# How the low part of 84 weight slabs is formed: a subtraction on GpSimd, or a transfer that adds onto the negated rounded weight

## The chip, the cores and the metric

The kernel runs on one core of a Trainium2 chip. The metric is the device time of one execution, in microseconds (us); the kernel before takes 781.51 us, the median of three runs. The engines are named as in the profile: PE (TensorE, matrix products; PEld is its weight load), DVE (VectorE), ACT (ScalarE), POOL (GpSimd) and SP (SyncE, which issues the loads and stores). A transfer between memories (DMA) runs on 16 DMA engines beside all of these.

## What is computed

One step of a network with a single layer, for 512 latent tokens and 128 prompt tokens, in float32:

```
h = rmsnorm(x, g_pre_mix) * (1 + scale1) + shift1
z = h @ w_in                       # 1024 -> 1792
q, k, v, lx, lg = split(z)
attn = attention(q, k, v)          # windowed, 8 heads over 2 kv heads, context and sink
lru  = (scan_forward + scan_backward of the gated conv of lx) * gelu(lg)
mix  = concat(attn, lru) @ w_out   # 1024 -> 1024
x = x + gate1 * rmsnorm(mix, g_post_mix)
h2 = rmsnorm(x, g_pre_mlp) * (1 + scale2) + shift2
f = square(relu(h2 @ mlp_w_up)) @ mlp_w_down     # 1024 -> 4096 -> 1024
x = x + gate2 * rmsnorm(f, g_post_mlp)
```

The six shifts, scales and gates are products of a conditioning vector with mod_w, 1024 x 6144. Each product of two float32 matrices is made of three products of rounded parts: with w = wh + wl and a = ah + al it is wh ah + wh al + wl ah, where wh is w rounded to the type float32r and wl = w - wh.

## The kernel before

The weights come from HBM as slabs of 128 x 1024 (512 KB), each by one load that SP issues, into one of five staging places (`st_ar`). `weight()` takes a slab, a place for the high part and one for the low part (`wh_ar`, `wl_ar`, three places each, four from the output projection on), has ACT or DVE round the slab into the first, and has an engine subtract: staging minus high part, rounded into the second (line 236). Then the staging place is free for the next load. For 84 slabs that engine is POOL; for the others it is DVE.

Where these 84 are used, in the order of the program:

- The start. The four tiles of the LRU input are slabs W0 to W3, called by `lx_weight`; W0, W1 and W3 have their low parts from POOL. The products go k tile by k tile (h0, h1, ... of the normalised, modulated input, rounded and split as well, line 220), three products for each k tile and LRU tile, between the products of the modulation sets a, b, s and t, which are short products whose results go through DVE to columns (transposes of 128x512 and multiplies of 128x8). In this section the table START is the strict order of the instructions on PE, DVE, ACT and SP; POOL's order is left to the scheduler.
- The middle. The input projection's further tiles (`z_tile`), attention and LRU, laid out by the list ORDER and, inside it, by the scheduler of the tile framework, which orders each engine's instructions. Six slabs have low parts from POOL. The LRU work has subtractions and multiplications on POOL of its own (lines 607, 648, 649, 693, 694).
- The output projection. Eight slabs for token tiles 0 to 2 (three of the low parts by POOL), then the eight again for token tiles 3 and 4 (all by POOL), two slabs at a time: for each token tile six products of 128x512 for a slab. Between them PE turns the finished token tiles (transposes of 128x128) for the MLP.
- The MLP. 4096 features in 32 tiles of 128, in groups of 4, 2 (twelve times) and 4: `up` takes a slab of w_up for each tile and makes 48 products from it, `down` a slab of w_down. The next group's `up` stands ahead of this group's `down`. All 64 low parts are POOL's.

All rounding and subtracting of weights is issued with high priority, which the scheduler takes into account. All products have the one helper line 194 in the profile, and are told apart by the tiles: `ps_z`, `ps_s`, `ps_t`, `ps_pv` are banks of the product memory, `rnd` holds the rounded parts, `big` all float32 data. `xt__108` and `yt__1186` are further memory for the start and the MLP.

## Time and profile before

| | us |
|---|---|
| three runs | 780.03, 781.51, 781.71 |
| median | 781.51 |
| span of the profiled execution | 778.3 |
| PE busy | 731.2 |
| DVE busy | 513.0 |
| ACT busy | 310.4 |
| POOL busy | 291.5 |
| of that, line 236 | 209.2 |

The span goes from the first to the last instruction that the profiler shows; of the profiled execution no other time is given beside it. Busy shares are means over stages of different kinds: a start with transfers at their most, a middle in which DVE and PE alternate, and an MLP from about 330 us to the end in which PE has products without a gap. The column "granted clock" of a stretch is what the chip gave TensorE, 1.00 being its upper level (2.4 GHz) and 0.50 its lower (1.2 GHz).

### The profile page before, as it was taken

Reading aid. Unit: us, or ns where it says so; the run is one execution under the profiler, and the core shown is the slowest. Engines: PE = TensorE matmul, PEld = TensorE weight load, DVE = VectorE, ACT = ScalarE, POOL = GpSimd, SP = SyncE. Lnnn points to the kernel's source line nnn. Section 1 sums busy time; section 2 is a strip of 40 time slices with the busy share of each in tenths; the row PEclk is TensorE's granted clock in tenths of the full one; section 3 lists DMA queues with packets and bytes.
Section 4 is the critical chain, followed back from the end, with each engine's and each line's share of the span. In section 5 each row is a group of like instructions: output and inputs, shape, how many; then the busy total and the mean of one; then the engine's idle time right before and its main releaser. Section 6 shows DMA issues by size and latency. Waiting matters only on the chain.

```text
span 778.3 us, 10655 instructions
## 1 busy us (share of the span) xinstructions
PE 731.2 (94%) x4170; PEld 618.7 (79%) x4170; DVE 513.0 (66%) x781; ACT 310.4 (40%) x596; POOL 291.5 (37%) x167
## 2 busy tenths in 40 slices
PE   6899997489899998999999999999999999999995
PEld 2577875466676786899899899899889889989884
DVE  4835699996967949886356655664675564462736
ACT  6435685355358565643032322222223123222222
POOL 2623437641412156433063242433323324232443
PEclk9999998889999999999999999999999999999998
DMA  9943724303201544313133223232333212211203
GB/s 341 405 182 122 256 97 158 108 1 108 84 28 55 205 173 136 109 55 113 50 129 116 82 87 104 81 120 70 106 112 101 88 55 82 82 55 55 82 0 135
DMA packets 26498, 88.09 MB, mean 113 GB/s; under 512 B 3104, under 2 KB 3792, under 8 KB 26448
## 3 DMA queue, kind: packets, MB, share of 16 engines
q1 hardware_dynamic: 26448, 87.41, 32.0%
q8 instruction: 32, 0.52, 0.3%
q14 instruction: 18, 0.15, 0.1%
HBM read 84.62 MB, written 2.78 MB: 112 GB/s over the span
## 4 chain that ended last, share of the span: by engine, by line
PE 72%; DVE 20%; ACT 5%; issue 2%; POOL 0%; DVEq 0%; ACTq 0%; POOLq 0%
PE ps_z L194 34%; PE ps_s L194 16%; DVE big L194 16%; PE ps_t L194 13%; PE ps_pv L194 8%; DVE rnd L194 3%; ACT big L194 2%; ACT rnd L194 1%; ACT xt__108 L194 1%; ACT L194 1%; DVE xt__108 L194 1%; POOL rnd L693 0%; DVE yt__1186 L194 0%; DVEq L1180 0%; DVEq L194 0%
## 5 line engine op out<-in xcount | busy, mean ns | idle before, releaser
L236 POOL TENSOR_TENSOR rnd<-big,rnd 128x1024 fp32r<-128x1024 f32 x84 | 209.2, 2503 | 382.5 <-ACT rnd L194 312.4
L194 PE MATMUL ps_z<-rnd 128*128 128x384 f32 (+3 forms) x2124 | 335.2, 314 | 5.0 <-ACT big L194 2.0
L194 PEld LDWEIGHTS ps_z<-rnd 128*128 128x128 f32 x2124 | 321.1, 190 | 16.9 <-issue 4.3
L194 ACT CAST rnd<-big 128x1024 fp32r<-128x1024 f32 (+8 forms) x159 | 125.9, 814 | 228.0 <-PE ps_pv L194 120.2
L194 DVE TENSOR_TENSOR big<-big 128x256 f32<-128x256 f32 (+8 forms) x139 | 145.9, 1057 | 105.0 <-ACT big L194 102.5
L194 PE MATMUL ps_s<-rnd 128*128 128x512 f32 (+4 forms) x464 | 116.5, 375 | 12.9 <-DVE rnd L194 8.3
L194 PEld LDWEIGHTS ps_s<-rnd 128*128 128x128 f32 x464 | 80.7, 194 | 36.3 <-issue 11.8
L194 ACT ACTIVATE big<-big 128x512 f32<-128x512 f32 (+9 forms) x129 | 75.4, 603 | 69.2 <-DVE big L194 66.0
L194 DVE TENSOR_TENSOR rnd<-big,rnd 128x384 fp32r<-128x384 f32 (+7 forms) x75 | 56.6, 765 | 16.8 <-ACT rnd L194 16.2
L194 PE MATMUL ps_s<-rnd,yt__1186 128*128 128x512 f32 (+1 forms) x252 | 65.8, 390 | 0.1
L194 PE MATMUL ps_t<-rnd 128*128 128x512 f32 (+1 forms) x240 | 61.7, 392 | 0.2 <-ACT big L194 0.2
L194 DVE SCALAR_TENSOR_TENSOR big<-big 128x644 f32<-128x644 f32 (+5 forms) x51 | 57.3, 1142 | 5.0 <-ACT big L194 3.9
L194 PE MATMUL ps_t<-rnd,yt__1186 128*128 128x512 f32 x216 | 56.8, 395 | 0.0
L194 ACT ACTIVATE big<-ps_z 128x384 f32<-128x384 f32 (+2 forms) x67 | 29.5, 441 | 63.6 <-PE ps_z L194 63.6
L194 PEld LDWEIGHTS ps_t<-rnd 128*128 128x128 f32 x240 | 44.8, 191 | 11.8 <-ACT big L194 1.3
L194 PEld LDWEIGHTS ps_s<-rnd,yt__1186 128*128 128x128 f32 x252 | 46.0, 188 | 10.1 <-ACT rnd L194 0.3
L194 DVE TENSOR_TENSOR big<-big,ps_s 128x512 f32<-128x512 f32 (+1 forms) x53 | 35.7, 674 | 18.5 <-PE ps_s L194 18.3
L194 PEld LDWEIGHTS ps_t<-rnd,yt__1186 128*128 128x128 f32 x216 | 40.5, 188 | 9.2
L194 DVE TENSOR_TENSOR big<-big,ps_t 128x512 f32<-128x512 f32 x52 | 35.3, 679 | 14.1 <-PE ps_t L194 14.1
L194 PE MATMUL ps_t<-big 128*128 128x128 f32 (+4 forms) x282 | 35.9, 311 | 7.1 <-DVE big L194 5.6
L194 PEld LDWEIGHTS ps_t<-big 128*128 128x128 f32 (+2 forms) x282 | 20.7, 129 | 21.7 <-issue 8.3
L194 ACT CAST yt__1186<-big 128x384 fp32r<-128x384 f32 (+1 forms) x32 | 14.7, 460 | 53.6 <-DVE big L194 53.6
(96 smaller groups left out, 576.4 us busy)
## 6 DMA issues: line engine op xcount, KB each, us to landing
big<-in_modw SPq DMA_DIRECT2D x32, 512.0 KB, 5.6
big<-in_wup SPq DMA_DIRECT2D x32, 512.0 KB, 3.2
big<-in_wdown SPq DMA_DIRECT2D x32, 512.0 KB, 3.2
big<-in_wout SPq DMA_DIRECT2D x16, 512.0 KB, 3.6
big<-in_win SPq DMA_DIRECT2D x14, 512.0 KB, 4.4
xt__108<-in_modw SPq DMA_DIRECT2D x8, 512.0 KB, 10.6
big<-in_modg SPq DMA_DIRECT2D x8, 512.0 KB, 3.3
big<-in_xT SPq DMA_DIRECT2D x8, 320.0 KB, 5.6
```

The lines of the kernel that those rows point to most:

```text
L194: i = f(*a, **k)
L236: (lo or pool).tensor_tensor(out=l.r, in0=s.f, in1=h.f, op=ALU.subtract)
```

## The change

For the 84 slabs whose low part was made by POOL, ACT writes the negated slab, rounded to float32r, into the low part's place, and POOL issues a transfer that reads the slab from staging and adds it to what stands there. Since rounding is the same for both signs, this leaves slab minus rounded slab. The high part is rounded as before, and the negated copy doesn't read it. The staging place is free once the transfer has read it. Low parts that DVE makes are left alone.

```diff
     def weight(src, hi, lo=None, places=None):
...
         with tc.high_priority():
             if hi == "d":
                 dve.tensor_copy(h.r, s.f)
             else:
                 act.copy(out=h.r, in_=s.f)
-            (lo or pool).tensor_tensor(out=l.r, in0=s.f, in1=h.f, op=ALU.subtract)
+            if lo is None or lo is pool:
+                act.activation(l.r, s.f, AF.Copy, scale=-1.0)
+                pool.dma_start(out=l.r, in_=s.f, accum_op=ALU.add)
+            else:
+                lo.tensor_tensor(out=l.r, in0=s.f, in1=h.f, op=ALU.subtract)
         s.free()
         return h, l
```

The rest of the diff removes comments, so that lines behind this one have numbers that are 4 higher. The scheduler lays the program out anew with it. In the rows below, a name in brackets is a semaphore that the instruction waits for: `DMAHW` a load that SP issued, `DMASW` a transfer that POOL issued, the others an engine.

On ACT, in the start, where the first slabs W0 and W1 have arrived; the casts of 128x640 are k tiles of h. Before:

```order
L194 CAST rnd<-big 128x1024 [waits DMAHW5_49]
L194 CAST rnd<-big 128x1024 [waits DMAHW6_49]
L194 CAST rnd<-big 128x640 [waits DVE_49] x4
L194 CAST rnd<-big 128x1024 [waits DMAHW3_49]
L194 CAST rnd<-big 128x1024 [waits DMAHW4_49,Activation_49]
```

and after:

```order
L194 CAST rnd<-big 128x1024 [waits DMAHW5_49]
L194 ACTIVATE rnd<-big 128x1024
L194 CAST rnd<-big 128x1024 [waits DMAHW6_49]
L194 ACTIVATE rnd<-big 128x1024
L194 CAST rnd<-big 128x640 [waits DVE_49] x4
L194 CAST rnd<-big 128x1024 [waits DMAHW3_49]
L194 CAST rnd<-big 128x1024 [waits DMAHW4_49,Activation_49]
L194 ACTIVATE rnd<-big 128x1024
```

Each of the slabs 0, 1 and 3 has got a negated copy behind its rounding, ahead of what ACT did next.

On POOL, at the same place; the memsets are borders of the LRU input tiles, and line 220 is the low part of a k tile of h. Before:

```order
L236 TENSOR_TENSOR rnd<-big,rnd 128x1024 [waits DMAHW5_49,Activation_49]
L236 TENSOR_TENSOR rnd<-big,rnd 128x1024 [waits DMAHW6_49,Activation_49]
L418 MEMSET big 128x2 [waits Pool_49]
L418 MEMSET big 128x3 x2
L418 MEMSET big 128x2
L220 TENSOR_TENSOR rnd<-big,rnd 128x640 [waits DMAHW2_49,Activation_49]
L236 TENSOR_TENSOR rnd<-big,rnd 128x1024 [waits DMAHW4_49,Activation_49]
```

and after:

```order
L238 DMA rnd<-big 128x1024 [waits DMAHW5_49,Activation_49]
L238 DMA rnd<-big 128x1024 [waits DMAHW6_49,Activation_49]
L220 TENSOR_TENSOR rnd<-big,rnd 128x640 [waits DMAHW2_49,Activation_49]
L238 DMA rnd<-big 128x1024 [waits DMAHW4_49,Activation_49]
L422 MEMSET big 128x2 [waits DMASW0_49]
L422 MEMSET big 128x3 x2
L422 MEMSET big 128x2
```

The subtractions have become issues; the memsets, which write over a freed staging block, have moved behind them and wait for the landing of a transfer.

On PE, at the end of the start, where `ps_z_261` and `ps_z_291` (in the new kernel `ps_z_263` and `ps_z_294`) are LRU tiles 2 and 3, `ps_s_391` and `ps_pv_423` (`ps_s_394`, `ps_pv_426`) the second token group of LRU tiles 0 and 1, and `ps_t_696` (`ps_t_700`) the products of modulation set 4. Before:

```order
L194 MATMUL ps_z_261<-rnd 128x384 x3
L194 MATMUL ps_z_291<-rnd 128x384 x3
L194 MATMUL ps_s_391<-rnd 128x258 x24
L194 MATMUL ps_pv_423<-rnd 128x258 x24
L194 MATMUL ps_t_696<-big 32x512 x3
L194 MATMUL ps_z_637<-rnd 128x384 x2
L194 MATMUL ps_t_696<-big 32x512 x2
L194 MATMUL ps_s_455<-rnd 128x258 x24
```

and after:

```order
L194 MATMUL ps_z_263<-rnd 128x384 x3
L194 MATMUL ps_z_294<-rnd 128x384 x3
L194 MATMUL ps_t_700<-big 32x512 x8
L194 MATMUL ps_s_394<-rnd 128x258 x24
L194 MATMUL ps_pv_426<-rnd 128x258 x24
L194 MATMUL ps_t_710<-big 32x8 x4
L194 MATMUL ps_z_641<-rnd 128x384 x2
L194 MATMUL ps_s_458<-rnd 128x258 x24
```

The eight products of set 4 stood in pieces behind the 48 products of LRU tiles 0 and 1, and stand ahead of them now.

On ACT in the MLP, where the slabs of a group of four come in. Before:

```order
L194 CAST rnd<-big 128x1024 [waits DMAHW4_49,PE_49,Pool_49]
L194 CAST rnd<-big 128x1024 [waits DMAHW5_49,PE_49,Pool_49]
L194 CAST rnd<-big 128x1024 [waits DMAHW0_49,PE_49,Pool_49]
L194 CAST rnd<-big 128x1024 [waits DMAHW3_49,PE_49,Pool_49]
L194 ACTIVATE big<-ps_z_3166 128x384 [waits PE_49]
```

and after:

```order
L194 ACTIVATE rnd<-big 128x1024 [waits DMAHW7_49,DMASW2_49,PE_49]
L194 CAST rnd<-big 128x1024 [waits PE_49]
L194 ACTIVATE rnd<-big 128x1024 [waits DMAHW0_49,DMASW3_49,PE_49]
L194 CAST rnd<-big 128x1024 [waits PE_49]
L194 ACTIVATE rnd<-big 128x1024 [waits DMAHW2_49,DMASW4_49,PE_49]
L194 CAST rnd<-big 128x1024 [waits PE_49,Activation_49]
L194 ACTIVATE rnd<-big 128x1024 [waits DMAHW3_49,DMASW5_49,PE_49]
L194 CAST rnd<-big 128x1024 [waits PE_49,Activation_49]
L194 ACTIVATE big<-ps_z_3198 128x384 [waits PE_49]
```

Each slab has two operations there instead of one, and the negated copy stands ahead of the rounding.

## Rows read from the trace of the kernel before

**Rows 1.** The page: busy us per engine, and PE's tenths in 40 slices

```profile
PE 731.2 (94%) x4170; PEld 618.7 (79%) x4170; DVE 513.0 (66%) x781; ACT 310.4 (40%) x596; POOL 291.5 (37%) x167
...
PE   6899997489899998999999999999999999999995
```

**Rows 2.** Stretches: length, busy PE, PEld, DVE, ACT, POOL, clock, DMA share, GB/s

```profile
0.00:40.00 40.00, 30.08 (x176) 17.25 (x178) 25.06 (x63) 21.56 (x30) 17.97 (x34) 1.00 0.97 374
...
120.00:160.00 40.00, 28.75 (x162) 23.90 (x155) 39.75 (x42) 19.58 (x32) 27.18 (x16) 0.80 0.31 108
440.00:480.00 40.00, 40.00 (x217) 36.16 (x216) 21.89 (x29) 9.88 (x15) 14.80 (x6) 1.00 0.23 76
```

**Rows 3.** Groups by line: busy us, mean ns of one, idle before

```profile
L236 POOL TENSOR_TENSOR rnd<-big,rnd 128x1024 fp32r<-128x1024 f32 x84 | 209.2, 2503 | 382.5 <-ACT rnd L194 312.4
...
L194 ACT ACTIVATE big<-big 128x1024 f32<-128x1024 f32 x7 | 7.6, 1084 | 1.9 <-DVE big L194 1.8
```

**Rows 4.** Order of time, POOL and DVE: start us, us, instruction [idle before]

```profile
18.80 4.69 POOL L236 TENSOR_TENSOR rnd<-big,rnd 128x1024 fp32r<-128x1024 f32 x2 [5.30 <-ACT rnd L194]
...
19.19 1.99 DVE L194 SCALAR_TENSOR_TENSOR big<-big 128x8 f32<-128x8 f32 x1
...
84.51 0.15 DVE L194 SCALAR_TENSOR_TENSOR big<-big 128x8 f32<-128x8 f32 x1
```

**Rows 5.** Order of time in the start, ACT and PE

```profile
17.67 1.04 ACT L194 CAST rnd<-big 128x1024 fp32r<-128x1024 f32 x1 [2.13 <-DMA big<-in_win]
18.96 1.05 ACT L194 CAST rnd<-big 128x1024 fp32r<-128x1024 f32 x1 [0.24 <-DMA big<-in_win]
22.25 0.72 ACT L194 CAST rnd<-big 128x640 fp32r<-128x640 f32 x1 [2.24 <-DVE big L194]
...
24.23 0.62 PE L194 MATMUL ps_z<-rnd 128*128 128x384 f32 x2 [0.76 <-DVE rnd L194]
24.68 0.69 PE L194 MATMUL ps_s<-rnd 128*128 128x384 f32 x3
```

**Rows 6.** The page's DMA issues: count, KB each, median us to landing

```profile
big<-in_wup SPq DMA_DIRECT2D x32, 512.0 KB, 3.2
...
xt__108<-in_modw SPq DMA_DIRECT2D x8, 512.0 KB, 10.6
```

**Rows 7.** The middle, POOL, DVE and PE in order of time; one stretch

```profile
127.81 5.72 POOL L236 TENSOR_TENSOR rnd<-big,rnd 128x1024 fp32r<-128x1024 f32 x2
...
128.51 2.16 DVE L194 SCALAR_TENSOR_TENSOR big<-big 128x8 f32<-128x8 f32 x1
...
131.19 2.88 DVE L194 TENSOR_TENSOR big<-big 128x512 f32<-128x512 f32 x1
...
143.00:149.00 6.00, 2.68 (x8) 2.71 (x9) 5.91 (x8) 0.00 (x0) 2.02 (x2) 0.50 0.00 0
...
146.32 1.62 PE L194 MATMUL ps_s<-rnd 128*128 128x384 f32 x4 [8.29 <-DVE rnd L194]
...
190.59 0.69 DVE L194 CAST rnd<-big 128x1024 fp32r<-128x1024 f32 x1
...
191.69 2.13 DVE L194 COPY big<-big 128x16 f32<-128x16 f32 x1 [0.34 <-PE ps_pv L194]
```

**Rows 8.** The output projection, PE in order of time

```profile
305.11 0.63 PE L194 MATMUL ps_z<-big 128*128 128x128 f32 x4 [2.65 <-DVE big L194]
...
312.00 2.96 PE L194 MATMUL ps_s<-rnd 128*128 128x512 f32 x12
```

**Rows 9.** The MLP, one pair of slabs: ACT, POOL, PE in order of time

```profile
417.88 2.00 ACT L194 CAST rnd<-big 128x1024 fp32r<-128x1024 f32 x2 [6.76 <-PE ps_pv L194]
...
419.01 4.76 POOL L236 TENSOR_TENSOR rnd<-big,rnd 128x1024 fp32r<-128x1024 f32 x2 [8.61 <-ACT rnd L194]
...
431.90 1.55 PE L194 MATMUL ps_s<-rnd 128*128 128x512 f32 x6
```

**Rows 10.** The end, PE in order of time

```profile
734.92 1.66 PE L194 MATMUL ps_s<-rnd 128*128 128x512 f32 x6 [1.39 <-DVE big L194]
```

## Prediction

> **What bounds the kernel now.** I read the busy totals first, then the stretches of 40 us, then the instructions in order of time at five places, and last the transfers. TensorE (PE) is busy 731.2 of 778.3 us, POOL 291.5, and the subtraction that goes is 209.2 of POOL's share, 84 of 2.5 us [rows 1, 3]. So POOL is not the bound, and most of what it gives back is free time on an engine that has enough of it. The page's line of 40 slices (19.5 us each) gives PE nine tenths or more in all slices from 311 us to the last [rows 1], and from 440 to 480 it is at 40.00 of 40.00 while POOL works a third of the time [rows 2]. A subtraction there is worth nothing unless it comes too late. What the edit can move is the 47 us that PE doesn't work, and these lie elsewhere: in the first two slices, in those from 117 to 311 us, and at the very end. From 39 to 117 us PE is at nine tenths or more too [rows 1], so a wait put in ahead of that stretch is paid in full. In 120 to 160 VectorE (DVE) is the full one, 39.75 of 40, PE works 28.75 and its clock is granted at 0.80 of full speed on average [rows 2].
>
> **What the subtraction costs today.** At 19.19 us DVE begins a multiply of 128x8 elements, which takes 0.15 us where POOL is idle, and it takes 1.99: it began while POOL was inside a weight subtraction and ended with it [rows 4]. At 128.51 the same happens (2.16), and of the 2.88 us of the operation at 131.19, 2.34 lie under the second of POOL's two subtractions, which end at 127.81 + 5.72 = 133.53 [rows 7]. At 191.69 even a copy of 16 columns takes 2.13 [rows 7]. So a DVE operation can stand still for as long as POOL subtracts. That is what there is to gain, and only where DVE is late.
>
> **The parts.** Each of the 84 slabs loses 2.5 us of POOL. It gains a negated, rounded copy on ScalarE (ACT), for which the 128x1024 activation at 1.08 us stands [rows 3], so 84 x 1.08 = 91 us on an engine that is busy 310 [rows 1]; and one transfer issued by POOL, which reads the slab and adds it in place. The kernel before issues no transfer from POOL and has none that adds. Its time from ACT's end to landing, call it L, is bounded by the nearest rows: 3.2 us for a slab of the same 512 KB that arrives in the MLP, 10.6 us for one in the crowded start [rows 6]. It cannot be below the first by any row, since it moves as many bytes and reads the destination too. I take 5 us in the MLP (3.2 and a second read of the slab: 512 KB at the 374 GB/s of the first stretch, 1.4 us, makes 4.6, and a little for POOL's issue) and 7 us in the start, the middle of the two ends, because transfers are 97% busy there [rows 2] but POOL's queue is not behind SP's loads. The Trainium skill gives a price of its own, on the page "DMA: Bandwidth & Descriptors" (Anatomy of one DMA): 2.0 us and the bytes at 436 GB/s, for a plain copy issued by GpSimd. By that estimate L would be 3.2 us, no low part of the start or the projection would be late, and the sum would come to 774 (1 - 3 - 4.2 - 1.4); no row here shows a transfer of that kind, and none that adds.
>
> *The start: 6 us lost (0 to 13).* Slabs 0 and 1 are rounded at 17.67 and 18.96, each 1.05 us [rows 5]. In the new order ACT negates each right behind its rounding, so the ends are 17.67 + 1.05 + 1.08 = 19.8 for slab 0 and 19.8 + 2.13 = 21.9 for slab 1. ACT's next task, rounding h, came at 22.25 [rows 5] and is not pushed. The low parts land at 19.8 + L and 21.9 + L, against 21.15 and 23.49, the middle and the end of the 4.69 us from 18.80, for the two subtractions [rows 4]. PE keeps its written order there, and the third product of k tile 0 reads the low part: it ran at about 24.5 for slab 0 and 25.1 for slab 1 [rows 5]. With L = 3.2 both are early; with 10.6 slab 1 is 32.5 - 25.1 = 7.4 us late, with 7 it is 3.8 late. PE has no slack after it, so 3.8 is lost. Behind it queue the products of modulation set b, and behind those DVE's next column step. On POOL a memset now waits for a landing, with the low parts of h's k tiles 5 to 7 behind it, which START has so much later that I put nothing. What an unlocked DVE returns at 19.19 lies ahead of the wait and is lost in it. Two things are added: a PE that stood still was given the lower of its two clock levels, 1.2 in place of 2.4 GHz (0.50 granted in 143 to 149, at the end of a gap of 8.29 us up to 146.32) [rows 7], for which I put 1.2 us (0 to 3.5); and the eight products of modulation set 4 now stand ahead of the 48 products of LRU tiles 0 and 1 instead of in pieces among them, so PE needs that set's slabs earlier: 1 us (0 to 2), by the 0.3 to 0.8 us that PE waited elsewhere in the start [rows 5]. That is 3.8 + 1.2 + 1.
>
> *The middle: 3 us gained (8 gained to 3 lost).* Six slabs of the input projection. In the stretch that DVE fills, 2.0 + 2.2 us of locks fall away [rows 7], and of the copy of 16 columns that took 2.13 at 191.69 I count half. With a shorter stretch at the lower clock (2.68 us of work at half speed, 1.3 of it given back) that makes 6.6 to 7.6. Against it stand six negations on ACT, which DVE waits for now and then, and a schedule that is laid out anew between 60 and 300 us: the same work, other neighbours, and POOL's own LRU products still lock DVE. I keep 3, somewhat less than half.
>
> *The output projection: 1 us lost (4 gained to 7 lost).* In its second half the slabs go two by two: 24 products for a pair, and twelve take 2.96 us [rows 8]. Before, PE waited 2.65 us at 305.11 for DVE [rows 8]: this, and some 1.5 of lower clock behind it, is the most to be gained, 4.2. Against it stands the time of a place. With four places a slab's place comes free 30 products, 30/12 x 2.96 = 7.4 us, before its next slab is used. In that time ACT rounds and negates and the transfer lands: 1.05 + 1.08 + L = 7.1 with L = 5. The spare 0.3 us goes to ACT's other work there (about 1 us an operation), so each of three pairs comes some 1 us late: 3 lost. Of the 4.2 I then keep 2. With L = 3.2 no pair is late and all 4.2 stands; with 7 each is late by 1.7 and some 0.6 more, 7 lost and nothing kept.
>
> *The MLP: nothing (0 to 27 lost).* 64 of the 84 slabs. A pair in the middle of it: two slabs rounded from 417.88 on, their subtractions done at 419.01 + 4.76 = 423.77, first use at 431.90 [rows 9]. New: each negation stands ahead of its rounding there, so the second ends 1.08 + 1.00 + 1.08 us behind 417.88, at 421.0, and its part lands at 421.0 + L, covered by the products that PE is still at until L = 10.9. If L were 13, each group would pay 2.1 us; the loop passes 13 times from a group of feature tiles to the next, so about 27. ACT is held by nothing new: a negation waits for the transfer that wrote its place before, and PE had to read that already.
>
> *The end: 1.4 us gained.* PE waited 1.39 us at 734.92 for DVE [rows 10], whose work there stood beside POOL's last subtractions. POOL's share of the output is untouched.
>
> Two rules bear on whether the lock really goes. The Trainium skill, page "SBUF — State Buffer" (Who interferes with whom), says that a DVE instruction with two inputs is held up by a GpSimd instruction that reads the memory, not by one that only writes it. The 1.99 us agree with its first half [rows 4]; no transfer issued by POOL is there for the second, by which the gains above would come in full. The other rule speaks against the change: the same section has copies and casts on DVE hold back GpSimd while it writes a transfer's descriptors. The longest cast of that kind in the rows takes 0.69 us [rows 7], so by it L would be up to 0.7 us longer, and the projection would lose 2 us more (3 x 0.7), inside its bounds.
>
> **Rivals.** *Faster: the locks decide.* If L is near 3.2 to 4 us even in the start, the start costs 1 us and the clock stays up, the middle gives 6, the projection 4, the end 1.4: -10.4, so 771. It decides from L of about 4 us down: 21.9 + 4 = 25.9, against the 25.1 at which PE comes to slab 1. For it: POOL's queue is its own, and DVE is full where the locks sit. Against it: at 374 GB/s and 97% the start has no spare transfer time [rows 2], and adding means reading twice.
> *Much slower: the transfer outlasts the MLP's cover.* One mechanism: a transfer that adds takes 16 engines for several microseconds, and L passes 10.9 us. Up to there the MLP hides all of it, beyond it 13 groups pay: at L = 13, 27 us there, 10 + 2 in the start and 7 in the projection, less 4.4 gained, 823. Against it: transfers are idle three quarters of the time in the MLP [rows 2].
> *It doesn't do what it says.* DVE is held by POOL's issuing as it was by subtracting, so that middle and end give back nothing, and what waits it brings are as long as those that it takes: 781.5.
>
> **How the numbers follow.** The execution that was profiled spans 778.3 us; the three timed runs lie 1.7 to 3.4 us above that (780.03 to 781.71, median 781.51), and I add to the median, since all terms lie inside the span. The sum is +6 - 3 + 1 + 0 - 1.4 = +2.6, so 784.1. Chances: forecast 0.45 (its own range 780 to 794), locks decide 0.33, cover outlasted 0.12, cancelled 0.10. The range goes from where the best ends of middle, projection and end add up (8 + 4 + 1.4, so 768) to where the worst of start, middle and projection do, less the end (13 + 3 + 7 - 1.4, so 803), and leaves out the much slower rival. About 0.2% (1.6 us) is what a measurement can tell from no change. Faster: 0.33 and 0.03 of the forecast's spread; same: 0.10 and 0.06 of it; slower: the other 0.36 of the forecast and 0.12. That is 0.36, 0.16, 0.48.
>
> **What would show it.** Right: PE waiting for a transfer that POOL issued between 24 and 32 us, landings 6 to 8 us after the issue there and 4 to 6 in the MLP, PE full from 330 to 720 us as before, no DVE operation of 128x8 above 0.3 us beside a weight slab, and a shorter gap at 138 to 146. Wrong: low parts in time at 25 us (then faster), or PE gaps at the start of each MLP group (then far slower).

## The result: 4.8% slower, and the profile after

The changed kernel takes 819.07 us (median, 816.08 to 819.87) against 781.15 for the kernel before (four runs, 780.03 to 781.71), a ratio of 1.0481 with a 95% interval of 1.0458 to 1.0503. That is 37.9 us slower, far outside the range of 768 to 803. The execution profiled here took 819.87 us and spans 817.4; that of before spans 778.3.

The page of the changed kernel: busy us per engine, PE's tenths and granted clock in 40 slices of 20.4 us, the two queues that matter (packets, MB, share of 16 engines' span), three groups (busy us, mean ns of one, idle before), and the adding transfers (count, KB each, median us from issue to landing). `q1` carries SP's loads, `q0` the transfers that POOL issues, and L238 is the adding transfer.

```profile
PE 745.2 (91%) x4170; PEld 628.9 (77%) x4170; DVE 409.9 (50%) x781; ACT 388.2 (47%) x680; POOL 154.4 (19%) x167
...
PE   6579985768999899699989999999999999999995
...
PEclk9699997877999899989999999999999999999998
...
q1 hardware_dynamic: 26448, 87.41, 29.4%
...
q0 software_dynamic: 12096, 44.05, 28.9%
...
L194 ACT ACTIVATE rnd<-big 128x1024 fp32r<-128x1024 f32 x84 | 88.7, 1056 | 156.6 <-PE ps_pv L194 149.8
...
L238 POOL DMA_DIRECT2D rnd<-big x84 | 73.5, 884 | 505.7 <-ACT rnd L194 291.8
...
L194 DVE TENSOR_TENSOR big<-big 128x256 f32<-128x256 f32 (+8 forms) x139 | 60.8, 442 | 144.1 <-ACT big L194 141.0
...
rnd<-big POOLq DMA_DIRECT2D x84, 512.0 KB, 5.3
```

The change did what it says. Against [rows 1], POOL lost 137 us and DVE 103, ACT gained 78, and the negation's price was right (1.06 us a slab; 1.08 was taken). The same group of DVE operations on two tensors read, in the page of before:

```profile
L194 DVE TENSOR_TENSOR big<-big 128x256 f32<-128x256 f32 (+8 forms) x139 | 145.9, 1057 | 105.0 <-ACT big L194 102.5
```

From 1057 ns to 442 for one: DVE no longer stands still beside the weight slabs (the lock, as the prediction calls it; POOL's own LRU products still hold it, as a run below shows). What got worse is the first half of PE's 40 slices. Its second and third slice are at 5 and 7 tenths where [rows 1] have 8 and 9, the sixth to ninth at 8, 5, 7 and 6 where they have 9, 7, 4 and 8, and a 6 stands in the seventeenth; the clock row has its lowest figures in the second slice (6) and in the seventh, ninth and tenth (7). From the eighteenth on PE is at 9, but for an 8 in the twenty-first and the 5 of the last.

The stretches of [rows 2] in the changed kernel (length; busy PE, PEld, DVE, ACT, POOL; granted clock, DMA share, GB/s):

```profile
0.00:40.00 40.00, 23.68 (x104) 11.17 (x104) 16.29 (x52) 21.43 (x28) 8.44 (x31) 0.83 0.97 341
120.00:160.00 40.00, 22.76 (x122) 14.55 (x122) 34.16 (x50) 26.36 (x43) 17.67 (x13) 0.79 0.42 134
440.00:480.00 40.00, 40.00 (x224) 35.66 (x223) 20.86 (x37) 16.93 (x25) 5.15 (x6) 1.00 0.74 188
```

In the first 40 us PE works 6.4 us less than before, at a mean clock of 0.83 in place of 1.00. From 440 to 480 it is at 40.00 of 40.00, as before, although the transfers' share went from 0.23 to 0.74.

The start in order of time, chosen lines of POOL, DVE, ACT and PE (start us, us, instruction, in brackets the idle time before it and what ended that):

```profile
20.24 0.17 DVE L194 SCALAR_TENSOR_TENSOR big<-big 128x8 f32<-128x8 f32 x1
...
21.04 1.02 POOL L238 DMA_DIRECT2D rnd<-big  x1 [6.51 <-ACT rnd L194]
22.93 0.87 POOL L238 DMA_DIRECT2D rnd<-big  x1 [0.87 <-DMA xt__108<-in_modw]
...
47.49 2.39 ACT L194 CAST rnd<-big 128x512 fp32r<-128x512 f32 x4 [14.14 <-DMA big<-in_gw]
...
29.64 0.69 PE L194 MATMUL ps_z<-rnd 128*128 128x384 f32 x1 [5.05 <-DMA rnd<-big]
...
33.52 0.69 PE L194 MATMUL ps_s<-rnd 128*128 128x384 f32 x1 [2.55 <-DMA rnd<-big]
...
48.79 0.44 PE L194 MATMUL ps_z<-rnd 128*128 128x384 f32 x1 [3.41 <-ACT rnd L194]
```

The multiply of 128x8 that took 1.99 us beside a subtraction [rows 4] takes 0.17. But PE stands 5.05 and 2.55 us for the landings of slabs 0 and 1, issued at 21.04 and 22.93. The third wait, 3.41 us at 48.79, is for ACT, and ACT had itself stood 14.14 us for `in_gw`, the LRU's gate weights: no slab of the change. On ACT the k tiles 4 to 7 of h stand behind that wait (the row at 47.49 merges the roundings of two gate weights and of two k tiles).

The middle, chosen lines of PE and ACT:

```profile
132.01 2.31 PE L194 MATMUL ps_z<-rnd 128*128 128x258 f32 x9 [11.96 <-ACT big L194]
...
122.58 3.00 ACT L194 ACTIVATE xt__108<-big 128x644 f32<-128x644 f32 x4
...
126.44 3.00 ACT L194 ACTIVATE big<-big 128x644 f32<-128x644 f32 x4
...
131.39 0.56 ACT L194 ACTIVATE big<-ps_z,big 128x384 f32<-128x384 f32 x1
```

PE has nothing to do for 11.96 us. It waits for ACT to empty a product bank (131.39), and that stands behind two runs of four LRU decays of 3 us each. The kernel before has the same decays, with the same evacuation behind them:

```profile
96.06 3.00 ACT L194 ACTIVATE xt__108<-big 128x644 f32<-128x644 f32 x4
...
99.93 3.00 ACT L194 ACTIVATE big<-big 128x644 f32<-128x644 f32 x4
...
104.94 0.57 ACT L194 ACTIVATE big<-ps_z,big 128x384 f32<-128x384 f32 x1
...
98.26 4.45 PE L194 MATMUL ps_z<-rnd 128*128 128x258 f32 x29
...
102.99 6.18 PE L194 MATMUL ps_z<-rnd 128*128 128x384 f32 x42
```

But there PE had products of the input projection beside them. No instruction on either side of that wait is one that the change touched: it comes with the new order. So two theories stood: that the landings decide (all 37.9 us are transfers that come too late), or that most of it is the order that the scheduler laid out anew.

### The profile page after: what moved, and what is told of

Same layout as the page of the kernel before. It is cut to its first block, busy times and chain, and to the rows that moved or that the text cites. A ratio compares the mean times of both kernels' runs of the same rounds, so it can differ in the third digit from the quotient of the medians.

```text
span 817.4 us, 10820 instructions
## 1 busy us (share of the span) xinstructions
PE 745.2 (91%) x4170; PEld 628.9 (77%) x4170; DVE 409.9 (50%) x781; ACT 388.2 (47%) x680; POOL 154.4 (19%) x167
## 3 DMA queue, kind: packets, MB, share of 16 engines
q1 hardware_dynamic: 26448, 87.41, 29.4%
q0 software_dynamic: 12096, 44.05, 28.9%
## 4 chain that ended last, share of the span: by engine, by line
issue 38%; PE 33%; DVE 10%; DMA 9%; POOL 5%; ACT 4%; SPq 1%; POOLq 0%; DVEq 0%; ACTq 0%
PE ps_z L194 18%; DVE big L194 7%; PE ps_s L194 6%; PE ps_t L194 5%; POOL rnd L238 4%; DMA rnd<-big 4%; PE ps_pv L194 3%; DVE rnd L194 2%; ACT big L194 2%; DMA big<-in_wup 1%; ACT rnd L194 1%; DMA big<-in_modw 1%; DMA big<-in_gw 1%; DMA xt__108<-in_modw 1%; SPq L194 1%
## 5 line engine op out<-in xcount | busy, mean ns | idle before, releaser
L194 PE MATMUL ps_z<-rnd 128*128 128x384 f32 (+3 forms) x2124 | 344.5, 319 | 30.6 <-ACT big L194 12.0
L194 PEld LDWEIGHTS ps_z<-rnd 128*128 128x128 f32 x2124 | 328.3, 193 | 42.8 <-ACT big L194 12.2
L238 POOL DMA_DIRECT2D rnd<-big x84 | 73.5, 884 | 505.7 <-ACT rnd L194 291.8
L194 ACT ACTIVATE rnd<-big 128x1024 fp32r<-128x1024 f32 x84 | 88.7, 1056 | 156.6 <-PE ps_pv L194 149.8
L194 DVE TENSOR_TENSOR big<-big 128x256 f32<-128x256 f32 (+8 forms) x139 | 60.8, 442 | 144.1 <-ACT big L194 141.0
L194 ACT ACTIVATE big<-ps_z 128x384 f32<-128x384 f32 (+2 forms) x67 | 29.2, 436 | 58.7 <-PE ps_z L194 58.7
L194 DVE TENSOR_TENSOR big<-big,ps_t 128x512 f32<-128x512 f32 x52 | 35.6, 685 | 24.9 <-PE ps_t L194 24.9
L194 DVE SCALAR_TENSOR_TENSOR big<-big 128x644 f32<-128x644 f32 (+5 forms) x51 | 45.5, 907 | 1.2
```

The lines of the kernel that those rows point to most:

```text
L194: i = f(*a, **k)
L238: pool.dma_start(out=l.r, in_=s.f, accum_op=ALU.add)
```

## The experiments

To part the two, the kernels below (all but the eleventh) name each engine's instructions in a fixed order, taken from the kernel before ("old order") or from the changed one ("new order"). With the old order, a negation stands right behind its slab's rounding on ACT (in the output projection, and where DVE rounds, the scheduler places it). A list `ADD` says which slabs are added by transfer: `start`, `z` (input projection), `out` (output projection), `mlp`. In these kernels the helper line of all products and ACT and DVE operations is L205 and the adding transfer L253. `hc` is the rounding that a negation is put behind, and `LAID` the table of the order.

```diff
-    def weight(src, hi, lo=None, places=None):
+    def weight(src, hi, lo=None, places=None, kind=""):
...
-            (lo or pool).tensor_tensor(out=l.r, in0=s.f, in1=h.f, op=ALU.subtract)
+            if (lo is None or lo is pool) and kind in ADD:
+                ng = act.activation(l.r, s.f, AF.Copy, scale=-1.0)
+                negs.append((ng.ins, hc.ins if hi != "d" and kind != "out" else None))
+                pool.dma_start(out=l.r, in_=s.f, accum_op=ALU.add)
+            else:
+                (lo or pool).tensor_tensor(out=l.r, in0=s.f, in1=h.f, op=ALU.subtract)
...
+    for e, code in LAID.items():
...
+        for a, b in zip(seq, seq[1:]):
+            tc.add_manual_dep(b, a.name, mybir.DependencyInfo(mybir.DependencyClass.NoSync,
+                                                              mybir.DependencyReason.DATA), reason="laid")
```

The times, beside runs of the kernel before on the same chip (781.32, 781.38 and 780.22 us for the kernels 1 to 4, 5 to 8 and 9 to 12; medians of four to ten executions, for kernel 9 of two):

| | order | added by transfer | us | ratio (95%) |
|---|---|---|---|---|
| 1 | old | all 84 | 792.01 | 1.0147 (1.0121 to 1.0173) |
| 2 | new | none | 807.12 | 1.0334 (1.0319 to 1.0350) |
| 3 | old | MLP | 784.27 | 1.0036 (1.0023 to 1.0050) |
| 4 | old | start | 791.20 | 1.0132 (1.0117 to 1.0147) |
| 5 | old | input projection | 773.79 | 0.9907 (0.9884 to 0.9931) |
| 6 | old | output projection | 783.51 | 1.0043 (1.0024 to 1.0062) |
| 7 | old | input projection, 60 of the MLP's | 770.51 | 0.9875 (0.9840 to 0.9909) |
| 8 | old | start, later loads held back | 790.19 | 1.0121 (1.0097 to 1.0145) |
| 9 | old | start, earlier loads held back | 798.28 | 1.0232 (1.0206 to 1.0258) |
| 10 | new, gate weights moved back | none | 798.54 | 1.0238 (1.0221 to 1.0255) |
| 11 | scheduler's own | as 7 | 777.95 | 0.9964 (0.9952 to 0.9976) |
| 12 | old | as 7, and the output projection's second half | 771.42 | 0.9890 (0.9873 to 0.9906) |

How late PE is, against the kernel before, when it begins its n-th product, in us (worked out from the start times of PE's products in the traces; the column "before" is the time in the kernel before; between 49 and 330 us the new order has other products at the same number). Each column is one execution. Kernels 5, 7 and 12 are the same up to the projection's second half, and at n = 900 they stand at -5.7, -4.0 and -5.3: differences of that size between columns say nothing. Naming the order costs nothing by itself: the column `mlp` is at 0.1 to 0.3 up to n = 1640, ahead of its own slabs.

```
   n  before  after  all,old  none,new  start    z    out    mlp  none,new,gates back
  90   25.77    9.2      8.3      -0.4    8.1  -0.2    0.2    0.3    0.0
 150   36.63   17.3      9.7       9.6    8.9  -0.2    0.2    0.3   -0.1
 600  101.38   13.9     11.5       6.6    8.9   1.4    0.2    0.3   -1.6
 630  106.38   26.2     11.5      18.9    8.9   1.4    0.2    0.3   10.7
1300  238.58   24.8      2.5      22.5   10.6  -7.5   -0.9    0.1   13.8
1450  268.00   29.7      8.3      26.6   10.6  -6.4    6.1    0.1   18.0
1640  313.85   29.2      9.4      26.2   10.6  -6.5    7.4    0.1   17.7
1860  348.76   35.3      6.8      27.6   10.6  -6.3    4.7   -2.3   18.9
2100  395.38   39.0      9.4      27.7   10.6  -6.4    4.7    0.4   19.1
3900  717.20   39.4      9.4      28.1   10.6  -6.4    4.7    0.4   19.5
3990  729.21   40.6     12.4      28.1   10.6  -6.4    4.7    3.5   19.5
4160  768.73   39.0     10.7      26.5   10.7  -6.4    4.7    1.8   17.9
```

**All 84 by transfer, in the old order.**

> All 84 low parts by a negated copy and an adding transfer, as in the changed kernel, but every engine takes its other instructions in the order of the kernel before; a negation stands right behind its rounding. Theory: the 38 us have two sources, late landings (some 11 us in the start with the lower clock behind them, 5 in the output projection, 3 in the MLP's first groups) and an order that the scheduler laid out anew (6 us for gate weights that ACT rounds ahead of a k tile of h, some 12 around 120 us), with a few us of locks given back. Then this kernel takes 790 us (785 to 798). Rival, landings alone: the order is innocent, 816 to 820. Rival, order alone: 775 to 783.

792.01 us, +10.7: inside the theory's range, and outside those of both rivals.

**The subtractions kept, in the new order.**

```diff
-    ADD = ('start', 'z', 'out', 'mlp')
+    ADD = ()
```

`LAID` holds the order of the changed kernel here.

> The reverse: POOL subtracts for all 84 slabs, no negation and no adding transfer, but every engine takes its instructions in the order of the changed kernel. Theory of two sources: 798 us (790 to 806), with a gap of PE of some 12 us around 110 us that the kernel before hasn't got. Rival, landings alone: 781 (779 to 784). Rival, order alone: 815 or more.

807.12 us, +25.8, a little above the theory's 806. Transfers and order alone make 10.7 + 25.8 = 36.5, of 37.9 measured together. So the order, with no transfer changed, is the larger part. Place by place the two don't add up so well: at n = 1640 the two kernels' columns add up to 35.6 us, and the changed kernel has 29.2; at n = 1860 it is 34.4 and 35.3. Between these the changed kernel's PE waits 3.84 us at 347.96 for ACT, which had itself waited for loads of w_up; in the kernel with subtractions that wait is 1.15. Two lines of this kernel's trace, ACT and PE:

```profile
39.52 2.39 ACT L205 CAST rnd<-big 128x512 fp32r<-128x512 f32 x4 [11.27 <-DMA big<-in_gw]
...
40.82 0.69 PE L205 MATMUL ps_z<-rnd 128*128 128x384 f32 x1 [7.34 <-ACT rnd L205]
```

Here too ACT stands for the gate weights with h's k tiles behind it, and PE waits 7.34 us. In the kernel before ACT rounded k tiles of h at 32.75 to 36.24, ahead of the gate weights at 39.94.

**The MLP alone.**

```diff
-    ADD = ('start', 'z', 'out', 'mlp')
+    ADD = ('mlp',)
```

> Only the 64 slabs of the MLP by negation and adding transfer, the 20 others by subtraction, everything in the order of the kernel before. Theory: PE hides the transfers but for the first groups: 781 us (778 to 785), with 1.4 us gained at the end and up to 4 lost between 330 and 440 us. Rival, the transfers outlast PE's cover in each group: 800 or more. Rival, the locks of the MLP were worth something: under 777.

784.27 us, +2.9 (+1.7 by the profiled span), inside. The table shows where: -2.4 at the entry (n = 1860), +2.7 near 392 us, +3.1 near 728 (which the theory hadn't), -1.7 at the end. Where it lost, POOL and PE:

```profile
387.59 0.86 POOL L253 DMA_DIRECT2D rnd<-big  x1 [24.96 <-PE ps_pv L205]
...
388.29 0.85 PE L205 MATMUL ps_z<-rnd 128*128 128x384 f32 x4 [0.58 <-ACT rnd L205]
390.18 0.50 PE L205 MATMUL ps_s<-rnd,yt__1186 128*128 128x512 f32 x1 [1.04 <-ACT rnd L205]
...
392.14 13.07 PE L205 MATMUL ps_z<-rnd 128*128 128x384 f32 x87 [0.53 <-DMA rnd<-big]
...
728.24 0.97 PE L205 MATMUL ps_s<-rnd 128*128 128x512 f32 x3 [1.06 <-DMA rnd<-big]
...
730.72 0.74 PE L205 MATMUL ps_s<-rnd 128*128 128x512 f32 x2 [1.51 <-DMA rnd<-big]
```

These are the slabs right behind a group of four. Four slabs hold all four places, so the next one's rounding waits for PE (POOL idle for 24.96 us, ended by PE). At the first place PE then waits 0.58 and 1.04 us for roundings, each of which now stands behind the negation of the slab before it on ACT, and 0.53 for a landing; at the second it waits 1.06 and 1.51, both for landings. The twelve groups of two are covered.

The entry gains because DVE isn't held there, as far as the traces tell. Two lines of the kernel before, and one of this kernel:

```profile
318.53 3.13 DVE L194 SCALAR_TENSOR_TENSOR big<-big 128x1024 f32<-128x1024 f32 x1
...
325.89 1.09 PE L194 MATMUL ps_t<-big 128*128 128x128 f32 x8 [1.23 <-ACT big L194]
```

```profile
316.98 1.28 DVE L205 SCALAR_TENSOR_TENSOR big<-big 128x1024 f32<-128x1024 f32 x1
```

The multiply took 3.13 us beside POOL's subtractions and takes 1.28; PE's wait of 1.23 us for ACT, and one of 0.68 for DVE ahead of it, are gone. No run parts this from the rest of the MLP.

**The start alone.**

```diff
-    ADD = ('start', 'z', 'out', 'mlp')
+    ADD = ('start',)
```

> Only the three slabs of the start by negation and adding transfer, in the order of the kernel before. Theory: PE waits some 8 us for the first two low parts and gets the lower clock for a while, 11 us, of which the waits of the stretch from 80 to 150 us take a little: 790 us (786 to 794). Rival, the transfers are slow only because of the new order's other loads: 782 (780 to 785).

791.20 us, +9.9, inside; the rival's 782 is out. PE's two waits, the landings' least, median and greatest, and the stretch behind the waits' begin (columns as for the stretches above):

```profile
28.57 0.69 PE L205 MATMUL ps_z<-rnd 128*128 128x384 f32 x1 [5.04 <-DMA rnd<-big]
...
32.43 0.69 PE L205 MATMUL ps_s<-rnd 128*128 128x384 f32 x1 [2.53 <-DMA rnd<-big]
...
DMA to landing us min/median/max: 8.5/9.1/10.5
...
24.00:34.00 10.00, 2.90 (x12) 1.31 (x12) 2.44 (x4) 4.49 (x5) 2.58 (x6) 0.63 1.05 309
```

The waits are those of the changed kernel to 0.02 us. They make 7.6 of the 8.9 us that PE is late at n = 150. The rest is put down to the clock: from 24 to 34 us 0.63 was granted on average, where before the whole first 40 us had 1.00 [rows 2]. Another 1.7 us come between n = 630 and 1300, and are not accounted for.

**The input projection alone.**

```diff
-    ADD = ('start', 'z', 'out', 'mlp')
+    ADD = ('z',)
```

> Only the six slabs of the input projection in the middle by negation and adding transfer, in the order of the kernel before. Theory: DVE no longer stands still beside their subtractions, and the transfers have cover, so the 7 us that the run of all 84 slabs in the old order gained between 120 and 225 us are gained here: 774 us (772 to 777). Rival: what was gained there was only its late start, made up in waits that the kernel before has as well: 780 to 782.

773.79 us, -7.6: the theory, to 0.2 us. Six of the 84 slabs make the kernel 0.9% faster. DVE and PE at the place of [rows 7], and its stretch:

```profile
128.29 2.67 DVE L205 SCALAR_TENSOR_TENSOR big<-big 128x8 f32<-128x8 f32 x1
...
131.48 0.68 DVE L205 TENSOR_TENSOR big<-big 128x512 f32<-128x512 f32 x1
...
143.03 1.62 PE L205 MATMUL ps_s<-rnd 128*128 128x384 f32 x4 [3.90 <-DVE rnd L205]
...
143.00:149.00 6.00, 5.97 (x26) 6.00 (x27) 5.97 (x9) 1.50 (x2) 1.85 (x1) 0.75 0.53 137
```

The operation of 2.88 us takes 0.68, PE's gap of 8.29 us is 3.90, and the clock in 143 to 149 is 0.75 in place of 0.50 [rows 7] (PE resumes 3.3 us earlier). A multiply of 128x8 still takes 2.67 us: POOL is in an LRU product of its own there, which the change leaves.

**The output projection alone.**

```diff
-    ADD = ('start', 'z', 'out', 'mlp')
+    ADD = ('out',)
```

> Only the eleven slabs of the output projection by negation and adding transfer, in the order of the kernel before. Theory: PE comes to the projection's first weights before their low parts have landed, 5 us lost near 240 us, and in the second half what late places cost and what locks give back cancel: 786 us (783 to 789). Rival, the loss seen there came from the other changes: 779 to 782.

783.51 us, +2.1, inside (ten executions from 782.15 to 788.14; the profiled one spans 782.8, +4.5). ACT, POOL and PE:

```profile
240.78 1.04 ACT L205 CAST rnd<-big 128x1024 fp32r<-128x1024 f32 x1
...
247.93 1.06 ACT L205 ACTIVATE rnd<-big 128x1024 fp32r<-128x1024 f32 x1
...
249.52 1.09 POOL L253 DMA_DIRECT2D rnd<-big  x1 [27.18 <-ACT big L205]
...
254.26 4.38 PE L205 MATMUL ps_z<-rnd,yt__1186 128*128 128x512 f32 x11 [3.98 <-DMA rnd<-big]
...
316.70 2.50 PE L205 MATMUL ps_t<-rnd 128*128 128x512 f32 x5 [2.81 <-DMA rnd<-big]
```

One negation of the first half came 7 us behind its slab's rounding, and PE waited 3.98 us for its landing; from 256 to 262 us the clock was 0.80, where the kernel before has 1.00. As far as the traces show, most of the 7 us isn't ACT's order: the subtraction of the kernel before had to wait for PE at this place as well,

```profile
246.70 2.38 POOL L236 TENSOR_TENSOR rnd<-big,rnd 128x1024 fp32r<-128x1024 f32 x1 [23.15 <-PE ps_s L194]
```

and was done 0.8 us ahead of the product that needs it, at 249.86. From the negation's begin at 247.93 to the landing it takes 6.3 us instead of 2.38. At 305.62 and 316.70 slabs of the second half are late by 1.03 and 2.81. By n = 1860 2.7 us have come back.

**What helps, without what hurts.** The input projection and the MLP, but for the two pairs behind groups of four:

```diff
-    ADD = ('start', 'z', 'out', 'mlp')
+    ADD = ('z', 'mlp')
...
-            ws.append(weight(wup[f], "a", kind="mlp"))
+            ws.append(weight(wup[f], "a", kind="mlp" if f not in (6, 7) else ""))
...
-        ws = [weight(wdown[f0 + i], "a", kind="mlp") for i in range(nf)]
+        ws = [weight(wdown[f0 + i], "a", kind="mlp" if f0 + i not in (26, 27) else "") for i in range(nf)]
```

> By negation and adding transfer: the six slabs of the middle and 60 of the MLP, all but the first weights that are used right behind a group of four (tiles 6 and 7 of w_up, 26 and 27 of w_down), which are subtracted like those of start and projection; order of the kernel before. Theory: the gains alone are left, 7 us in the middle, 2.3 between 320 and 341 us, 1.7 at the end: 770.5 us (768 to 774). Rival, the waits move to the next slabs of the MLP: 775 to 780.

770.51 us, as expected: 1.25% faster than the kernel before, the lowest median of all that ran.

**Why a landing in the start takes 8.5 to 10.5 us.** Two kernels, from that of the start alone. The first makes the loads that are issued after the first two adding transfers wait until those have landed (`adds` lists the adding transfers, and SP issues its loads in order):

```diff
-                sp.dma_start(out=b.f, in_=modw[st, c])
+                ld = sp.dma_start(out=b.f, in_=modw[st, c])
+                if st == 2 and c == 0:
+                    tc.add_manual_dep(ld.ins, adds[1].name, mybir.DependencyInfo(
+                        mybir.DependencyClass.Sync, mybir.DependencyReason.DATA), reason="after the second landing")
```

> As the run with the start's three slabs alone, but SP issues the 2 MB of modulation set s, and all behind them, only when the second adding transfer has landed. Theory: the landings are late since these loads share the 16 engines: they come 5 to 6.5 us behind their issue instead of 8.5 and 10.5, PE goes on near 27 us instead of 33, and set s is late by some 3 to 6 us instead: 786 to 792 us in all. Rival, an adding transfer takes that long there whatever runs beside it: landings unchanged and 795 or more.

The landings stayed (least, median, greatest), and from 26 to 30 us the transfers were as full as ever (the column before the last, 1.06):

```profile
DMA to landing us min/median/max: 8.5/9.6/10.4
...
26.00:30.00 4.00, 1.23 (x3) 0.82 (x3) 0.71 (x1) 1.04 (x1) 1.23 (x5) 0.56 1.06 245
```

The second landing came after 9.6 us instead of 10.5, the first after 8.5 as before (the 10.4 are the third's). The theory's landings of 5 to 6.5 us are out, and the 790.19 us lie in its range by luck; the rival's 795 or more is out as well. What was issued ahead was still draining, so this did not settle it. The second holds back the loads of set b, issued ahead of the adding transfers, and all behind them (`held[0]` is set b's first load):

```diff
+    tc.add_manual_dep(held[0], adds[1].name, mybir.DependencyInfo(
+        mybir.DependencyClass.Sync, mybir.DependencyReason.DATA), reason="after the second landing")
```

> As the run with the start's three slabs alone, but SP issues the 2 MB of modulation set b, and all the loads behind them, only when the second adding transfer has landed, so that few transfers are left ahead of the adding ones. It is made for the landings, not for the time, since PE then waits for set b instead. Theory: the landings of the start are late because of the backlog of loads that SP has issued ahead of them: now 4.5 to 6 us from issue to landing. Rival: an adding transfer takes its 8.5 to 10.5 us there whatever runs beside it.

```profile
DMA to landing us min/median/max: 4.7/5.5/9.8
...
20.00:24.00 4.00, 0.00 (x0) 0.00 (x0) 3.10 (x6) 2.82 (x5) 1.49 (x2) 0.58 0.76 146
```

4.7 and 5.5 us, and the third, issued later in the crowd, 9.8. Since holding back the later loads alone did little, a landing in the start is long because the adding transfer shares the 16 engines with the loads that were issued before it. The kernel as a whole is slower by this (798.28), since set b comes late.

**The gate weights put back.** The new order, with the two gate weight roundings on ACT and their low parts on POOL moved behind the last k tile of h. As rows of the order, first ACT's (128x640 are k tiles of h, 128x512 the gate weights), then POOL's:

```diff
-L205 CAST rnd<-big 128x512
-L205 CAST rnd<-big 128x640
-L205 CAST rnd<-big 128x512
-L205 CAST rnd<-big 128x640 x3
+L205 CAST rnd<-big 128x640 x4
+L205 CAST rnd<-big 128x512 x2
...
+L231 TENSOR_TENSOR rnd<-big,rnd 128x640 x3
 L231 TENSOR_TENSOR rnd<-big,rnd 128x512 x2
-L231 TENSOR_TENSOR rnd<-big,rnd 128x640 x3
```

> As the run with subtractions in the new order, but the rounding on ACT and the subtraction on POOL of two gate weights stand behind k tiles 4 to 7 of h again, as in the kernel before. Theory: these four instructions alone cost the 10 us that PE lost at 36 us in that run: 797.5 us (795 to 801) against 807.1. Rival, the 10 us come from the loads or another engine's order: 803 to 808.

798.54 us, inside. The new order costs 18.3 us then, instead of 25.8. Of what is left, the table shows 12.3 us between n = 600 and 630, the gap at the decays, which stands here as well:

```profile
116.48 4.65 PE L205 MATMUL ps_z<-rnd 128*128 128x258 f32 x24 [11.97 <-ACT big L205]
```

and 4.2 between 1300 and 1450, where PE waits three times for ACT and DVE, 3.6 us in all, the longest 2.20 at 265.46. An order with that evacuation ahead of the decays and all else as in the new one wasn't tried: that the 12 us come from its place, and not from another of the order, is read from the trace and not shown by a run.

**The order left to the scheduler.** The edit of the fastest kernel, but no order prescribed:

> The same choice of slabs as the run with the middle and most of the MLP (66 by negation and adding transfer, 18 subtracted), but laid out by the scheduler alone, with no order prescribed. Theory: the choice is worth 11 us in the old order, and the scheduler, whose order of the changed kernel cost 26 us with subtractions, gives an order of its own again, good or bad: 770 to 800 us, with the difference to 770.5 showing as gaps of PE ahead of 320 us, none in the MLP. Rival, the scheduler's order is harmed only by the slabs of start and projection: 769 to 773.

777.95 us: 0.4% faster than before, and about 7 us slower than the same edit in the old order; the range held, and the rival's 773 is out. The place was not as expected: of what PE is later than in the old order, 1.7 us lie ahead of 314 us (n = 1640), and 3.9 more come at the entry of the MLP, where PE waits 1.52 us at 330.52 for ACT and 0.65 at 331.79 for DVE and has a clock of 0.72 from 332 to 338. One edit thus has two times, by the order that comes with it.

**The second half of the output projection added.**

```diff
-                ws = [weight(wout[k], "a", kind="out") for k in ks]
+                ws = [weight(wout[k], "a", kind="out2") for k in ks]
```

> As the run with the middle and most of the MLP in the old order, with the eight slabs of the projection's second half by negation and adding transfer too. Theory: late places and returned locks cancel there: 770.5 us (768 to 774), with PE waiting for a transfer near 305 or 316 us. Rival, what that half gave back in the run of the projection alone (2.7 us by 340 us) comes on top: 766 to 768.

771.42 us, as the theory says: nothing gained and nothing lost that the measurement can tell. PE waits 3.68 us at 303.71 for a landing; its wait of 2.68 us for DVE, at 299.27 in kernel 7, is gone.

## Why the prediction was wrong, by its own steps

**What bounds the kernel, and the lock.** Right. The MLP was full but for the slabs behind its groups of four, and DVE's locks beside the weight slabs went. The DVE operations with two inputs fell from 1057 to 442 ns once POOL issued instead of reading two inputs of its own. The Trainium skill ("SBUF — State Buffer", Who interferes with whom) has a DVE instruction with two inputs held up by a GpSimd instruction that reads the memory, and the trace agrees. Its rule against the change, that DVE's casts hold back GpSimd's descriptors, weighs little here: an issue took 0.85 us at least, 0.88 in the mean and 1.61 at most.

**The start (6 us, 0 to 13).** The mechanism was right and the term mis-sized. L was 8.5 and 10.5 us where 7 was taken. PE's second wait was put at 3.8 us in all; the two came to 7.6, and the start alone makes +9.9. The bound of 13 held. 7 was the middle between a free load and a crowded one, taken because POOL's queue is not behind SP's loads; but with the loads ahead of them held back the same landings took 4.7 and 5.5 us, so they did stand behind those loads. The row with the crowd, 10.6 [rows 6], was the one of this place. Set 4, put at 1 us, cost nothing that the traces show.

**The middle (3 us gained, 8 gained to 3 lost).** This step failed, and it carries the miss. The locks gave back 7.6 us by the medians and 6.5 by the spans (771.8 against 778.3), where 6.6 to 7.6 were worked out from rows. What was set against them in one clause, "a schedule that is laid out anew between 60 and 300 us: the same work, other neighbours", was not the 4 us or so for which half was kept, but 25.8 us. Of these 7.5 (25.8 against 18.3 with the gate weights put back) come from the start, where the sum had nothing for a new order, and some 12 from the gap at the decays. Two places of it were there to be read. In the changed order the gate weights' rounding stood ahead of h's k tiles on ACT (the table START orders only what it names, and that rounding is not in it), and the wait for `in_gw` in front of it was in the trace of before, 2.97 us at 39.94. And at the decays, 12 us of ACT's work without a break, the new order has no product left for PE. The prediction looked at where the edited instructions had moved, and not at where the others had.

**The output projection (+1, -4 to +7).** +2.1 for it alone (+4.5 by the span), inside. The second half went as the sum has it: 1.03 and 2.81 us of waiting, where 3 were taken, against what DVE gave back. The first half, for which the sum had nothing, lost 3.98 us and some clock, where a place comes free 3 us before its slab is used.

**The MLP (0).** L was right: 5 was taken, and 5.2 is the median of the fastest kernel (4.4 to 9.3). The cover of the pairs was right as well: no group of two paid. The rival's threshold of 10.9 us wasn't put to the test by a pair: the longer landings (11.1 us in kernel 3, up to 11.5 in the changed one) were of slabs that come in fours. But the pair that was worked out [rows 9] was not the tightest. Behind a group of four the next slab has no place until PE is nearly there; this cost 2.7 and 3.1 us, and at the first of the two places 1.62 of the 2.15 us of waiting were for roundings on ACT, where the sum says that "ACT is held by nothing new". The 2.4 us at the entry were not in the sum either.

**The end (1.4 gained).** 1.7 us, right.

**The rivals.** "The locks decide" described the middle rightly, and its condition (L of 4 us in the start) was false. "Much slower" gave 823, near the time measured by chance, for a mechanism that no run shows: PE was at 40.00 of 40.00 between 440 and 480. Added up from the kernel with all 84 in the old order, the parts are: start 9.7, middle -7.2, projection 6.9, entry of the MLP -2.6, inside it 2.6 and 3.0, end -1.7, which is 10.7; that is the sum to be set against the predicted +2.6, which held some 4 us for the new order besides. The other 27 us are put down to the order, 25.8 of them shown by the kernel that keeps the subtractions.

## What to carry to other kernels

Where a scheduler lays the program out, an edit has two effects, its own and that of the new order: build the edit in the old order, and the old operations in the new order, before saying what the edit does. Before a time is predicted, the rows that moved without having been edited deserve as much care as the edited ones, above all a wait for a load that has come ahead of something urgent, and a long run on one engine that has lost its cover on another. And an edit that is applied to all of a kind is best judged place by place: here six slabs out of 84 carried most of the gain, and in the old order three carried most of the loss.

## What the runs showed of the hardware that was not expected

A transfer that adds takes about twice the engines' time of a load for each byte: 44.05 MB of them took 28.9% of the 16 engines, and 87.41 MB of loads 29.4% (the two queue lines of the changed kernel's page). No adding transfer of a 512 KB slab landed in less than 4.4 us in any run. By the Trainium skill's figures for a transfer that GpSimd issues ("DMA: Bandwidth & Descriptors", Anatomy of one DMA) a plain one of that size would take an estimated 3.2 us; none ran here.

Its landing depends on what was issued ahead of it on other queues, and little on what came after: 8.5 and 10.5 us behind the loads of the start, 8.5 and 9.6 with later loads held back, and 4.7 and 5.5 us with the loads ahead of it held back too.

Issuing costs POOL 0.88 us and DVE next to nothing, where the subtraction it replaces cost POOL 2.50 us [rows 3] and held DVE for up to as long. Worked out from the two traces: 102 DVE operations of the changed kernel that overlapped an issue, and no other work of POOL's, took 0.3 us longer in all than the median of their like with POOL idle; 127 that overlapped a weight subtraction in the kernel before took 102 us longer. So the same edit gains where DVE is late and loses where its own landing is.
